# Zero-padded query tiles for the 64-wide heads of a two-layer hybrid trunk

## Chip, cores and metric

The kernel runs on one core of one Trainium2 chip. The metric is the device time of one execution in microseconds; before the change it is 2455.56 us, the median of 3 runs (2454.08 to 2456.77).

## The reference, cut to what matters

Two layers of an encoder trunk work on 512 prompt frames and 32 sample frames with a model width of 1024. A layer is a SwiGLU block, a mixer with three groups of attention heads side by side, a second SwiGLU block and a gated embedding. The mixer projects its normed input once and splits it:

```python
qa, ka, va, cq, ckv, kr, qc, kc, vc, fl = jnp.split(xn @ w_in, SPLITS, axis=-1)
qa, ka, va = (a.reshape(bsz, t, H_A, HEAD_DIM) for a in (qa, ka, va))     # 4 heads x 64
qc, kc, vc = (a.reshape(bsz, t, H_C, HEAD_DIM) for a in (qc, kc, vc))     # 4 heads x 64
...
z = jnp.einsum('bqhd,bkhd->bhqk', q, k).astype(jnp.float32) * SB_SCALE    # group A
z = jnp.einsum('bqhd,bkhd->bhqk', q, k).astype(jnp.float32) * MLA_SCALE   # group B, 96 wide, 8 heads
z = jnp.einsum('bqhd,bkhd->bhqk', q, k).astype(jnp.float32) * FOX_SCALE   # group C, plus a bias of forget gates
```

Group A is stick-breaking attention, B latent attention, C attention with forget gates. The scores of a head of A or C are sums over 64 products. Prompt frames see only earlier frames (or chunks), so a block of 128 queries needs 128, 256, 384 or 512 keys.

## The kernel before, in words

Activations lie transposed, features on partitions and the 544 frames along the row; the frames are worked on in two halves of 256 and 288 (HALVES). A projection (gemm, L238 to L240) is done as three passes over high and low parts of inputs and weights: each of 8 chunks takes three matmuls, so 24 for a half.

In the mixer, class QK projects 128 columns of W_in at a time, which are two heads of Q or of K, one head on partitions 0 to 63, the other on 64 to 127. VectorE evicts the result from PSUM with the norm's factor into one "m" buffer of 128x544 (L531 for K, L533 for Q, which also scales), ScalarE copies the sample frames to a small tile (L109, h<-m), and K is written out by a DMA that GpSimd issues (L537). Pool "m" has 14 buffers in this phase; besides Q and K of A and C it holds the latents of B (four tiles of cq, two of ckv), B's queries and parts of the normed output. A buffer is given to the next tile when all readers of its last one are done.

attend_qk takes the rows of each head out of the pair's tiles and calls attend_pair, which works on blocks of 128 queries. For each of the two heads it issues the score product (L395), for C a bias product (L401), the mask as a bf16 product with an identity (L402), the softmax or stick-breaking weights (soft, on ScalarE and VectorE), transposes (L135) and the product with V (L414). In A and C the score product of the second head is held in program order (hold); B's is not. B's heads have 128-row tiles of their own: 64 rows of content, 32 rotary rows and their 32 swapped ones. So L395 stands for 64-row products in A and C and 128-row products in B, all in float32. A float32 product shows up as two MATMUL records.

The program is written in dataflow form; a planner with modelled durations chooses the order on each engine and places the waits. Program order around the change: Q and K of A's first pair, its attention, Q and K of A's second pair, small projections, Q and K of C's first pair, A's second attention, C's first attention, Q and K of C's second pair, C's second attention, then B. The planner mixes projections, as far as they are ready, between the attention's products.

Of the kernel before, what the change touches and what calls it, by code (L numbers as in the profile page):

```python
# [12 lines left out]
ALU = mybir.AluOpType  # L13
# [5 lines left out]
SEQ = 512  # L19
DEC = 32  # L20
T = SEQ + DEC
# [14 lines left out]
def trunk(ctx: ExitStack, tc, a, outs, depth=2):  # L36
    nc = tc.nc
# [19 lines left out]
    def tl(tag, shape, dt=F32):  # L57
        count[0] += 1
        tag = alias.get(tag, tag)
        p, n = where[tag]  # L60
        return p.tile(shape, dt, tag=tag, name=f"{tag}_{count[0]}", bufs=n)
# [29 lines left out]
    unit = lambda tag, dt=F32: tl(tag, [128, T], dt)  # L91
# [5 lines left out]
    hold = tc.keep_in_program_order  # L97
# [4 lines left out]
    tt = nc.vector.tensor_tensor  # L102
    stt = nc.vector.scalar_tensor_tensor
    ts = nc.vector.tensor_scalar
    mm = nc.tensor.matmul
    f = lambda ap: ap.bitcast(F32)

    def copy(out, in_):
        act(out, in_, AF.Copy)  # L109
# [23 lines left out]
    def transpose(out, in_):  # L133
        n = in_.shape[0]
        nc.tensor.transpose(out, in_, ident[0:n, 0:n])  # L135
# [89 lines left out]
    def split_w(raw, k, n, parts=1):  # L225
        th, tlo = ring[wn[0] % len(ring)]
        wn[0] += 1
        hi, lo = tl(th, [128, k, n], F32R), tl(tlo, [128, k, n], F32R)
        for b in (slice(k * i // parts, k * (i + 1) // parts) for i in range(parts)):
            split(hi[:, b, :], lo[:, b, :], raw[:, b, :])  # L230
        return hi, lo

    def gemm(p, w, xh, xl, cols, order=None):
        wh, wl = w
        ks = order or list(range(len(xh)))
        c0, c1 = cols
        for i, k in enumerate(ks):
            mm(p, wh[k], xh[k][:, c0:c1], start=i == 0, stop=False)  # L238
            mm(p, wh[k], xl[k][:, c0:c1], start=False, stop=False)  # L239
            mm(p, wl[k], xh[k][:, c0:c1], start=False, stop=i == len(ks) - 1)  # L240

    def wk(w, n=128):
        return tuple([x[:, i, 0:n] for i in range(x.shape[1])] for x in w)
# [136 lines left out]
    def attend_pair(cb, kind, heads, o, chunk, vget, extra=None):  # L380
        identb = cb[:, 0:128]
        mask = cb[:, 128 * ("ABC".index(kind) + 1):128 * ("ABC".index(kind) + 2)]
        if chunk not in o:
            o[chunk] = unit("y")
        for b in range(2):
            cols = slice(b * 256, b * 256 + 256)
            O = tl("pv", [128, 256])
            pts = [tl("pb" if b else "pa", [128, 2 + 2 * b, 256]) for _ in heads]
            lqs = [extra(hd, cols) for hd, _ in heads] if extra else None
            for i in (2 * b, 2 * b + 1):  # L390
                nk, q0 = (i + 1) * 128, i * 128
                w = max(nk, 256) if extra else nk
                ss = [bank("acc") for _ in heads]
                for e, (_, (q, k)) in enumerate(heads):
                    one = mm(ss[e][:, 0:w], q[:, q0:q0 + 128], k[:, 0:w], start=True, stop=False)  # L395
                    if e and kind != "B":
                        hold(one)
                for e, s in enumerate(ss):
                    if extra:
                        lq, rk = lqs[e]  # L400
                        mm(s[:, 0:w], lq[0:100, q0 - b * 256:q0 - b * 256 + 128], rk[0:100, 0:w], start=False, stop=False)  # L401
                    mm(s[:, q0:nk], identb, mask, start=False, stop=True)  # L402
                    P = soft(kind, s[:, 0:nk], nk)
                    t = bank("tr")
                    for j in range(i + 1):
                        transpose(t[:, j * 128:j * 128 + 128], P[:, j * 128:j * 128 + 128])
                    qq = slice((i % 2) * 128, (i % 2) * 128 + 128)
                    (copy if e else nc.vector.tensor_copy)(pts[e][:, 0:i + 1, qq],
                                                           t[:, 0:nk].rearrange("p (j s) -> p j s", s=128))
            end = 2 * b + 1  # L410
            for j in range(end + 1):
                qs = slice(128 if j == end else 0, 256)
                for e, (hd, _) in enumerate(heads):
                    one = mm(O[64 * e:64 * e + 64, qs], vget(hd, j), pts[e][:, j, qs], start=j == 0, stop=j == end,  # L414
                             skip_group_check=True)
                    if j or e:
                        hold(one)
            (copy if b else nc.vector.tensor_copy)(o[chunk][:, cols], O)

    def soft(kind, S, nk):  # L420
        P = tl("t", [128, nk])
        if kind == "A":
            act(P, S, AF.Abs)
            act(P, P, AF.Exp, scale=-1.0)
            act(P, P, AF.Ln, bias=1.0)
            stt(P, S, 0.0, P, op0=ALU.max, op1=ALU.add)
            nc.vector.tensor_tensor_scan(P[:, ::-1], ones_row(0, 128, nk), P[:, ::-1], 0.0, op0=ALU.mult, op1=ALU.add)
            tt(P, S, P, op=ALU.subtract)
            act(P, P, AF.Exp)
        else:  # L430
            mx, sm = col(), col()
            nc.vector.reduce_max(mx, S, axis=AX.X, negate=True)
            act(P, S, AF.Exp, bias=mx, accum_out=sm)
            nc.vector.reciprocal(sm, sm)
            act(P, P, AF.Copy, scale=sm)
        return P
# [42 lines left out]
    def mix(l, h, x, g_next):  # L479
# [27 lines left out]
        sn = tl("h", [128, 8, DEC])  # L507
# [4 lines left out]
        def proj(col0):  # L512
            return wk(load_w(a["w_in"][l, UNITS.index(col0)], KD, 128))
# [3 lines left out]
        class QK:  # L517
            def __init__(s, col0, scale, slot, dst=None):
                s.col0, s.scale, s.slot, s.dst, s.w = col0, scale, slot, dst, None

            def half(s, i, pbank=prj):
                c0, c1 = HALVES[i]
                if s.w is None:
                    s.w = proj(s.col0)
                    s.kf = unit("m")
                n = c1 - c0
                p = pbank()[:, 0:n]
                gemm(p, s.w, x.xh, x.xl, (c0, c1))
                t = s.kf[:, c0:c1]
                if s.scale == 1.0:  # L530
                    tt(t, p, x.r(c0, c1), op=ALU.mult)  # L531
                else:
                    stt(t, p, s.scale, x.r(c0, c1), op0=ALU.mult, op1=ALU.mult)  # L533
                if c1 == T:
                    copy(sn[:, s.slot, :], s.kf[:, SEQ:T])
                    if s.dst is not None:
                        nc.gpsimd.dma_start(out=s.dst, in_=s.kf)  # L537

        def qk_jobs(qcol, kcol, scale, slot, dst):
            return [(QK(qcol + 128 * c, scale, slot + c),  # L540
# [30 lines left out]
        def attend_qk(kind, js, c, chunk, v, extra=None):  # L571
            q, k = js[c]
            heads = []
            for e in range(2):
                r = slice(e * 64, e * 64 + 64)
                heads.append((2 * c + e, tuple(z.kf[r, 0:SEQ] for z in (q, k))))
            attend_pair(cb, kind, heads, o, chunk, v.get, extra)

        def cache_kv(kname, vname):
# [71 lines left out]
        w = wk(split_w(raw, KD, 68), 68)  # L651
        for c0, c1 in HALVES:
            n = c1 - c0
            p = bank("prj")[0:68, 0:n]
            gemm(p, w, x.xh, x.xl, (c0, c1))
            t, u = tl("q", [128, n]), tl("q", [128, n])
# [4 lines left out]
            fx, e = t[64:68, :], u[64:68, :]  # L661
# [14 lines left out]
        w = proj(CKV)  # L676
        ckh, ckl, ckf = unit("m", F32R), unit("m", F32R), unit("kf")
        cks = unit("r")
        for c0, c1 in HALVES:
            p = bank("prj")[:, 0:c1 - c0]  # L680
# [7 lines left out]
        for c0, c1 in HALVES:  # L688
            R = tl("q", [128, c1 - c0])
# [5 lines left out]
        for c0, c1 in HALVES:  # L695
            R = tl("q", [128, c1 - c0])
# [147 lines left out]
        def attend_b(hp, q, k):  # L844
            heads = [(2 * hp + e, (q[e][:, 0:SEQ], k[e][:, 0:SEQ])) for e in range(2)]
            attend_pair(cb, "B", heads, o, 2 + hp, lambda hd, j: vb[j][:, hd * 64:hd * 64 + 64])
# [53 lines left out]
    def ple_inputs(l):  # L900
        ph, pl = ([unit("ph", F32R) for c in range(2)] for _ in range(2))
        for c in range(2):
            raw = unit("raw")
            nc.sync.dma_start(out=raw, in_=a["p"][l, c * 128:c * 128 + 128, :])
            split(ph[c], pl[c], raw)
        return ph, pl
# [87 lines left out]
    with phase(FFN, FFN_RING):  # L994
        h, x = start()
        x = ffn1(0, h, x)
    for l in range(depth):
        with phase(MIX, MIX_RING):
            h, x = mix(l, h, x, gains[l]["g_ff2_pre"])
        alias["h"], alias["y"] = alias.get("y", "y"), alias.get("h", "h")  # L1000
        with phase(FFN, FFN_RING):
            p = []
            x = ffn(h, x, a["w_ff2_gu"][l], a["w_ff2_down"][l], gains[l]["g_ff2_post"], gains[l]["g_ple_pre"], False,
                    lambda: p.extend(ple_inputs(l)))
            x = ple(l, h, x, gains[l + 1]["g_ff1_pre"] if l + 1 < depth else None, p)
            if l + 1 < depth:
                x = ffn1(l + 1, h, x)
# [99 lines left out]
```

## Time and profile before

| what | before |
|---|---|
| median of 3 runs | 2455.56 us |
| profiled execution | 2452.86 us, span 2451.1 us |
| granted TensorE clock, mean | 0.985 of full speed |
| PE (matmuls) | 2382.6 us, 97% of the span |
| PEld (weight loads, beside PE) | 2253.3 us, 92% |
| DVE (VectorE) | 1379.4 us, 56% |
| ACT (ScalarE) | 1025.6 us, 42% |
| POOL (GpSimd) | 48.8 us, 2% |

The span is the time from the first to the last instruction in the profiled execution; what lies outside it is 1.8 us. Matmuls overlap, and the profile models their ends, so the time that a matmul takes is better read from one start to the next than from its duration. The mixer of the first layer lies at 430 to 690 us and that of the second at about 1650 to 1910 us, in the same order of work.

### The profile page before, as it was taken

Reading aid. Unit: us, or ns where it says so; the run is one execution under the profiler, and the core shown is the slowest. Engines: PE = TensorE matmul, PEld = TensorE weight load, DVE = VectorE, ACT = ScalarE, POOL = GpSimd, SP = SyncE. Lnnn points to the kernel's source line nnn. Section 1 sums busy time; section 2 is a strip of 40 time slices with the busy share of each in tenths; the row PEclk is TensorE's granted clock in tenths of the full one; section 3 lists DMA queues with packets and bytes.
Section 4 is the critical chain, followed back from the end, with each engine's and each line's share of the span. In section 5 each row is a group of like instructions: output and inputs, shape, how many; then the busy total and the mean of one; then the engine's idle time right before and its main releaser. Section 6 shows DMA issues by size and latency. Waiting matters only on the chain.

```text
span 2451.1 us, 43918 instructions
## 1 busy us (share of the span) xinstructions
PE 2382.6 (97%) x18022; PEld 2253.3 (92%) x18022; DVE 1379.4 (56%) x3052; ACT 1025.6 (42%) x2163; POOL 48.8 (2%) x116
## 2 busy tenths in 40 slices
PE   8999999999998999999999999999999989999997
PEld 8999999886688999999999999998865989999997
DVE  6344446765757344446863444476667663444466
ACT  5322224566754322224533222245677543222243
POOL 0000000110000000000000000001100000000000
PEclk9999999999998999999999999999999999999998
DMA  5322322222023322322213223122211233323221
GB/s 160 111 81 86 105 70 72 93 88 59 23 80 107 104 88 83 101 85 87 84 47 96 95 80 102 54 94 86 89 51 44 81 94 105 95 75 104 81 70 37
DMA packets 72376, 204.99 MB, mean 84 GB/s; under 512 B 9248, under 2 KB 18088, under 8 KB 72176
## 3 DMA queue, kind: packets, MB, share of 16 engines
q1 hardware_dynamic: 69072, 193.57, 25.4%
q0 software_dynamic: 3104, 8.62, 1.1%
q8 instruction: 141, 2.31, 0.4%
q14 instruction: 59, 0.48, 0.1%
HBM read 188.21 MB, written 11.85 MB: 82 GB/s over the span
## 4 chain that ended last, share of the span: by engine, by line
PE 92%; DVE 4%; DMA 2%; ACT 1%; issue 0%; SPq 0%; DVEq 0%; ACTq 0%
PE acc L238 12%; PE acc L239 12%; PE acc L240 12%; PE prj L238 10%; PE prj L239 10%; PE prj L240 10%; PE pv L238 4%; PE pv L239 4%; PE pv L240 4%; PE acc L395 3%; PE pv L414 2%; PE tr L135 2%; DMA raw<-in_w_ff_gu_dram 1%; DVE z L303 1%; PE prj L556 1%; PE prj L557 1%
## 5 line engine op out<-in xcount | busy, mean ns | idle before, releaser
L109 ACT ACTIVATE wh<-raw 128x1024 fp32r<-128x1024 f32 (+3 forms) x157 | 151.1, 965 | 247.5 <-PE acc L239 108.1
L109 ACT ACTIVATE wx<-raw 128x1024 fp32r<-128x1024 f32 (+3 forms) x149 | 139.5, 936 | 266.4 <-PE acc L239 100.2
L113 DVE TENSOR_TENSOR wl<-raw,wh 128x1024 fp32r<-128x1024 f32 (+3 forms) x157 | 173.6, 1107 | 80.0 <-ACT wh L109 79.3
L113 DVE TENSOR_TENSOR wx<-raw,wx 128x1024 fp32r<-128x1024 f32 (+3 forms) x149 | 159.4, 1070 | 75.1 <-ACT wx L109 74.9
L238 PE MATMUL prj<-xa,wh 128*128 128x256 f32 (+3 forms) x632 | 187.8, 297 | 4.6 <-DVE q L346 2.7
L239 PE MATMUL prj<-xb,wh 128*128 128x256 f32 (+3 forms) x632 | 187.1, 296 | 4.1 <-DVE xb L259 4.1
L109 ACT ACTIVATE m<-q 128x256 fp32r<-128x256 f32 (+1 forms) x192 | 81.9, 431 | 255.0 <-DVE q L349 252.7
L240 PE MATMUL prj<-xa,wl 128*128 128x256 f32 (+3 forms) x632 | 184.3, 292 | 0.0
L238 PE MATMUL acc<-xa,wx 128*128 128x256 f32 (+1 forms) x600 | 174.4, 291 | 5.7 <-ACT wx L109 5.7
L239 PE MATMUL acc<-xb,wx 128*128 128x256 f32 (+1 forms) x600 | 173.8, 290 | 0.0
L240 PE MATMUL acc<-xa,wx 128*128 128x256 f32 (+1 forms) x600 | 173.4, 289 | 0.0
L239 PE MATMUL acc<-xb,wh 128*128 128x288 f32 (+1 forms) x576 | 167.4, 291 | 0.0
L240 PE MATMUL acc<-xa,wl 128*128 128x288 f32 (+1 forms) x576 | 166.8, 290 | 0.0
L238 PE MATMUL acc<-xa,wh 128*128 128x288 f32 (+1 forms) x576 | 166.6, 292 | 0.0
L240 PE MATMUL prj<-xa,wx 128*128 128x288 f32 (+1 forms) x480 | 139.5, 291 | 1.3 <-DVE wx L113 1.3
L238 PE MATMUL prj<-xa,wx 128*128 128x288 f32 (+1 forms) x480 | 140.6, 293 | 0.0
L239 PE MATMUL prj<-xb,wx 128*128 128x288 f32 (+1 forms) x480 | 140.3, 292 | 0.0
L347 ACT ACTIVATE q<-q 128x256 f32<-128x256 f32 (+1 forms) x176 | 74.1, 425 | 143.3 <-DVE q L346 140.8
L239 PEld LDWEIGHTS prj<-xb,wh 128*128 128x128 f32 (+1 forms) x632 | 120.1, 190 | 7.7 <-DVE xb L259 5.9
L238 PEld LDWEIGHTS prj<-xa,wh 128*128 128x128 f32 (+1 forms) x632 | 120.1, 190 | 7.7 <-DVE q L346 3.2
L240 PE MATMUL acc<-xa,wy 128*128 128x288 f32 (+1 forms) x424 | 122.7, 289 | 0.7 <-DVE wy L113 0.7
L238 PE MATMUL acc<-xa,wy 128*128 128x288 f32 (+1 forms) x424 | 123.3, 291 | 0.0
(500 smaller groups left out, 7802.5 us busy)
## 6 DMA issues: line engine op xcount, KB each, us to landing
raw<-in_w_ff_gu_dram SPq DMA_DIRECT2D x174, 512.0 KB, 3.5
raw<-in_w_ff_down_dram SPq DMA_DIRECT2D x64, 384.0 KB, 3.1
raw<-in_w_ff_down_dram SPq DMA_DIRECT2D x64, 320.0 KB, 2.9
raw<-in_w_in_dram SPq DMA_DIRECT2D x22, 512.0 KB, 3.5
raw<-in_w_out_dram SPq DMA_DIRECT2D x16, 512.0 KB, 3.4
raw<-in_w_ple_gate_dram SPq DMA_DIRECT2D x16, 512.0 KB, 3.4
raw<-in_w_v_dram SPq DMA_DIRECT2D x8, 512.0 KB, 3.4
t<-dh SPq DMA_DIRECT2D x16, 144.0 KB, 3.0
```

What stands on the lines that cost most here:

```text
L109: act(out, in_, AF.Copy)
L113: tt(lo, src, f(hi), op=ALU.subtract)
L135: nc.tensor.transpose(out, in_, ident[0:n, 0:n])
L238: mm(p, wh[k], xh[k][:, c0:c1], start=i == 0, stop=False)
L239: mm(p, wh[k], xl[k][:, c0:c1], start=False, stop=False)
L240: mm(p, wl[k], xh[k][:, c0:c1], start=False, stop=i == len(ks) - 1)
L303: stt(t, s.y[c][:, c0:c1], s.g[c], s.R[c0], op0=ALU.mult, op1=ALU.mult)
L347: act(g, g, AF.Silu)
L395: one = mm(ss[e][:, 0:w], q[:, q0:q0 + 128], k[:, 0:w], start=True, stop=False)
L414: one = mm(O[64 * e:64 * e + 64, qs], vget(hd, j), pts[e][:, j, qs], start=j == 0, stop=j == end, skip_group_check=True)
L556: mm(p, x.xh[k][:, c0:c0 + n], s.wh[k], start=k == 0, stop=False)
L557: mm(p, x.xl[k][:, c0:c0 + n], s.wh[k], start=False, stop=False)
```

## The change

Q of A and C gets a tile for each head instead of one for the pair. The head's 64 rows are written by the eviction, the other head's 64 rows are set to zero by a GpSimd memset. K keeps one tile for the pair. The score product of a head is then the product of its padded Q with the whole K tile, over 128 rows. The eviction of Q becomes two instructions of 64 partitions, the copy of the sample frames too. The hold on the second head's score product goes.

```diff
@@ attend_pair
                 for e, (_, (q, k)) in enumerate(heads):
-                    one = mm(ss[e][:, 0:w], q[:, q0:q0 + 128], k[:, 0:w], start=True, stop=False)
-                    if e and kind != "B":
-                        hold(one)
+                    mm(ss[e][:, 0:w], q[:, q0:q0 + 128], k[:, 0:w], start=True, stop=False)
@@ class QK
             def __init__(s, col0, scale, slot, dst=None):
                 s.col0, s.scale, s.slot, s.dst, s.w = col0, scale, slot, dst, None
+                s.rows = [slice(0, 64), slice(64, 128)] if dst is None else [slice(0, 128)]
 
             def half(s, i, pbank=prj):
                 c0, c1 = HALVES[i]
                 if s.w is None:
                     s.w = proj(s.col0)
-                    s.kf = unit("m")
+                    s.kf = [unit("m") for _ in s.rows]
+                    if len(s.rows) == 2:
+                        for e in range(2):
+                            nc.gpsimd.memset(s.kf[e][s.rows[1 - e], 0:SEQ], 0.0)
                 n = c1 - c0
                 p = pbank()[:, 0:n]
                 gemm(p, s.w, x.xh, x.xl, (c0, c1))
-                t = s.kf[:, c0:c1]
-                if s.scale == 1.0:
-                    tt(t, p, x.r(c0, c1), op=ALU.mult)
-                else:
-                    stt(t, p, s.scale, x.r(c0, c1), op0=ALU.mult, op1=ALU.mult)
-                if c1 == T:
-                    copy(sn[:, s.slot, :], s.kf[:, SEQ:T])
-                    if s.dst is not None:
-                        nc.gpsimd.dma_start(out=s.dst, in_=s.kf)
+                R = x.r(c0, c1)
+                for t, r in zip(s.kf, s.rows):
+                    if s.scale == 1.0:
+                        tt(t[r, c0:c1], p[r, :], R[r, :], op=ALU.mult)
+                    else:
+                        stt(t[r, c0:c1], p[r, :], s.scale, R[r, :], op0=ALU.mult, op1=ALU.mult)
+                    if c1 == T:
+                        copy(sn[r, s.slot, :], t[r, SEQ:T])
+                if c1 == T and s.dst is not None:
+                    nc.gpsimd.dma_start(out=s.dst, in_=s.kf[0])
@@ attend_qk
             for e in range(2):
-                r = slice(e * 64, e * 64 + 64)
-                heads.append((2 * c + e, tuple(z.kf[r, 0:SEQ] for z in (q, k))))
+                heads.append((2 * c + e, (q.kf[e][:, 0:SEQ], k.kf[0][:, 0:SEQ])))
```

## Rows read from the trace of the kernel before

**Rows 1.** The page: busy time, share and instructions of each engine.
```profile
PE 2382.6 (97%) x18022; PEld 2253.3 (92%) x18022; DVE 1379.4 (56%) x3052; ACT 1025.6 (42%) x2163; POOL 48.8 (2%) x116
```

**Rows 2.** Busy time by stretch: length, engines, granted clock, DMA share, GB/s.
```profile
480.00:515.00 35.00, 35.00 (x270) 32.94 (x268) 27.26 (x54) 18.61 (x36) 6.77 (x23) 1.00 0.26 80
...
537.00:567.00 30.00, 30.00 (x186) 21.31 (x185) 15.67 (x36) 18.16 (x45) 1.27 (x3) 1.00 0.24 70
...
640.00:690.00 50.00, 44.44 (x260) 30.62 (x260) 41.01 (x119) 38.95 (x110) 0.00 (x0) 0.97 0.14 46
```

**Rows 3.** Waits of weight loads, 440 to 600 us: total us, times, longest.
```profile
PEld tr L135 <- ACT t L424: 1.1, 2, 0.5
...
PEld acc L395 <- DVE m L531: 0.2, 1, 0.2
```

**Rows 4.** The score line's records: min/median/max ns, starts, shapes.
```profile
L395 PE MATMUL acc<-m,m x128: 272/481/694, 456.4 to 1805.2; 64*128 64x256 f32 x48, 64*128 64x384 f32 x32, 64*128 64x512 f32 x32, 64*128 64x128 f32 x16
...
L395 PE MATMUL acc<-xb,m x128: 271/484/648, 593.3 to 1878.3; 128*128 128x128 f32 x32, 128*128 128x256 f32 x32, 128*128 128x384 f32 x32, 128*128 128x512 f32 x32
```

**Rows 5.** Timeline of PE, a 64-row product: start us, us, instruction.
```profile
459.63 0.28 PE L238 MATMUL prj<-xa,wh 128*128 128x256 f32 x1
459.83 0.70 PE L395 MATMUL acc<-m,m 64*128 64x256 f32 x2
460.46 0.23 PE L402 MATMUL acc<-cb 128*128 128x128 bf16 x1
...
460.70 0.28 PE L240 MATMUL prj<-xa,wl 128*128 128x256 f32 x1
```

**Rows 6.** Timeline of PE, a 128-row product of group B.
```profile
614.66 0.29 PE L240 MATMUL prj<-m,wl 128*128 128x288 f32 x1
614.80 0.59 PE L395 MATMUL acc<-xb,m 128*128 128x256 f32 x2
615.23 0.22 PE L402 MATMUL acc<-cb 128*128 128x128 bf16 x1
...
615.46 0.28 PE L768 MATMUL prj<-m,wh 128*128 128x256 f32 x1
```

**Rows 7.** Timeline of PE, group C: through score and bias to the mask.
```profile
548.17 0.28 PE L240 MATMUL prj<-xa,wl 128*128 128x256 f32 x1
...
549.23 0.23 PE L402 MATMUL acc<-cb 128*128 128x128 bf16 x1
...
570.62 0.28 PE L401 MATMUL acc<-rk,lq 100*128 100x256 f32 x1
570.75 0.23 PE L402 MATMUL acc<-cb 128*128 128x128 bf16 x1
```

**Rows 8.** Timeline of PE, two heads' products that start together.
```profile
569.19 0.70 PE L395 MATMUL acc<-m,m 64*128 64x256 f32 x4
569.83 0.50 PE L767 MATMUL prj<-wh,m 128*128 128x512 f32 x1
```

**Rows 9.** Timeline of PE, group B, from mask to mask over 384 columns.
```profile
605.39 0.22 PE L402 MATMUL acc<-cb 128*128 128x128 bf16 x1
...
606.15 0.22 PE L402 MATMUL acc<-cb 128*128 128x128 bf16 x1
```

**Rows 10.** Single instructions on VectorE, ScalarE and GpSimd, by line and shape.
```profile
L533 DVE SCALAR_TENSOR_TENSOR m<-prj,r x14: 418/450/459, 452.8 to 1766.7; 128x288 f32<-128x288 f32 x8, 128x256 f32<-128x256 f32 x6
...
L801 DVE COPY xb<-prj x16: 425/425/427, 579.6 to 1838.3; 64x256 f32<-64x256 f32 x16
...
L109 ACT ACTIVATE h<-m x8: 212/212/225, 453.7 to 566.3; 128x32 f32<-128x32 f32 x8
...
L645 POOL MEMSET bq<- 128x512 f32 x2 | 1.1, 548 | 0.0
```

**Rows 11.** Timelines of PE and VectorE: A's last score, C's next Q.
```profile
534.55 1.12 PE L395 MATMUL acc<-m,m 64*128 64x512 f32 x2
...
542.37 0.42 DVE L533 SCALAR_TENSOR_TENSOR m<-prj,r 128x256 f32<-128x256 f32 x1 [1.00 <-PE prj L240]
```

## The prediction

> **What bounds the kernel now.** I read the page's busy times first, then busy time by stretch, then the waits of TensorE's weight loads, then the score line and the timeline around single products. The page shows TensorE's matmuls (PE) busy for 2382.6 of 2451.1 us, VectorE for 1379.4 and GpSimd for 48.8 [rows 1]. Busy time alone doesn't prove a bound, so look where the change lies: the scores of groups A and C, at 456 to 587 us in the first layer and 1675 to 1805 us in the second. There PE is busy 35.00 of 35.00 and 30.00 of 30.00 us, while VectorE has 27.26 and 15.67 and ScalarE 18.61 and 18.16 [rows 2]. Only after 640 us does PE have holes: 44.44 of 50. The weight loads' waits between 440 and 600 us agree: the largest that another engine ends is 1.1 us in two pieces, and the evictions of Q and K make a score wait once, for 0.2 us [rows 3]. So in the stretch of the change the end of the layer is set by how fast PE gets through its own list, and what a score product takes there goes to the end of the span.
>
> **The scores, 64 rows against 128.** The score line has 128 MATMUL records on 64 rows (64 products of two records, 32 in a layer) and as many on 128 rows, those of group B, which multiply the same float32 shapes over all rows [rows 4]. So the trace of before holds the price of both forms.
>
> Take 256 columns. On 64 rows, from the start of the projection matmul ahead to the start of the second projection matmul behind: 459.63 to 460.70, 1.07 us [rows 5]. The same chain on 128 rows: 614.66 to 615.46, 0.80 us, and the matmul ahead has 288 columns there, not 256, which is 0.01 us more [rows 6]. So 64 rows cost 0.28 us more for the same product. Where it lies can be seen in the steps: the product starts 0.20 us after the matmul ahead instead of 0.13 to 0.14, and takes 0.63 us to the mask's product instead of 0.43. I read it as a fixed charge for going into 64-row form, between its two passes and out again, where a weight load finds no matmul to hide behind, and so take it for all widths.
>
> Where forget-gate scores go straight into the bias product (10 of 16 products of C in a layer), the charge runs on: 548.17 to 549.23 is 1.06 us up to the mask's product; in 128-row form it would be 0.12 for the matmul ahead, 0.43 for the product [rows 6] and 0.13 from bias to mask, 0.68 in all. That is 0.38, so 0.10 more than above [rows 7].
>
> I went through the timeline product by product. Of the 32 of a layer 4 stand in two pairs, where the heads' four records start together: the pair of 256 columns takes 0.64 us from its start to the next matmul [rows 8], with about 0.11 us of going in. Two 128-row products take 2 x 0.43 = 0.86: a loss of 0.11. The pair of 128 columns gains some 0.06. Together -0.05 in a layer. The other 28 products run alone.
>
> Eight of these 28 follow the short bf16 mask product. There 128 rows have a charge too: 605.39 to 606.15 is 0.76 us, less 0.055 for the mask and 3 x 0.215 for 384 columns leaves 0.06 [rows 9]. I take 0.05 off for each.
>
> Sum for a layer: 28 x 0.28 = 7.84; + 10 x 0.10 = 1.0; - 8 x 0.05 = 0.4; - 0.05: 8.4 us. Two layers: 16.8 us. The ends: 0.19 us for each of 28 (the steps inside the product alone) is 10.6; 0.38 for every one of them is 21.3.
>
> **What is added elsewhere.** Each of the four Q tiles of a layer is now evicted by two VectorE instructions on 64 partitions in place of one on 128, in both halves: 16 more in both layers. An instruction on 64 partitions is no shorter (0.425 us for 64x256, against 0.418 to 0.459 for Q's own), so 16 x 0.44 = 7.0 us, and ScalarE gets 8 more copies of 0.21 us, 1.7 us [rows 10]. VectorE's idle share in these stretches hides them; if the projections' PSUM banks came free later and PE ran out of others, they would cost up to 7.0. The nearest row says almost nothing: the existing evictions hold up a score for 0.2 us [rows 3]. I take 0.5 us, ends 0 and 7.0. If the softmax chains behind them became the bound, the price is the same 7.0.
>
> The zeros are 16 GpSimd memsets of 64x512; the nearest is 128x512 in 0.548 us, so 8.8 us on GpSimd [rows 10]. What is queued behind them there is output and cache DMA issue. GpSimd idles nearly all the time [rows 1], and the first zeros are wanted at 456.4 us [rows 4], some 25 us after the mixer has begun. Cost 0, upper end 8.8 if every one stood ahead of a score; below nothing it can't be.
>
> The dropped program-order hold on the second head's score only gives the planner more freedom. The trace can't price a new order; nearest are group B's scores, which have no hold and start the same way, in 0.13 us behind a projection [rows 6]. I take 0, and plus or minus 3 us.
>
> Sum against the profiled execution's own 2452.86 us: 2452.9 - 16.8 + 0.5 = 2436.6. The runs' median is 2.7 above that execution (2455.56), so 2439.3 us is the forecast, 16.3 us less.
>
> A rule speaks against it. The Trainium skill, TensorEngine Tiling (Key Properties and When to Use Tiling), says that a product over at most 64 rows should use half the array's rows, since two such tiles can run in parallel, up to twice as fast. The trace agrees for the 4 pairs that start together [rows 8], but the other 56 products have nothing in the other half, and there half the rows is the dearer form.
>
> **Rivals.**
> 1. Half of it doesn't arrive. In C's stretch PE's work is more entangled with the softmax: 30.00 busy, but VectorE has just been given more. If C's gain (14 x 0.28 + 1.0 = 4.9 us a layer) becomes waiting, 2439.3 + 9.8 = 2449. Against it: both other engines are idle over a third of that stretch [rows 2].
> 2. No change: evictions uncovered (7.0), and a rewritten order that leaves the remaining 9 us in the holes after 640 us, where PE waits already [rows 2]. About 2455. For it: the order of everything is planned anew; against it: nothing of the change lies in that stretch.
> 3. Slower: the buffers. Fourteen buffers hold Q, K and the latents ("m"). A Q now takes two. When C's second pair is projected, there would be 4 + 2 latents, 3 of C's first pair, 3 of A's second and 3 new ones: 15. If A's second pair isn't done by then, the projection of C's second pair must wait and can't fill PE beside C's first attention. That projection is 2 x 2 x 24 matmuls of 0.12 to 0.13 us, 12.1 us a layer; uncovered in both layers, 24.2 - 16.3: 2463. It decides from the moment at which the first of these Q's evictions comes before A's last scores. In the trace A's last score product starts at 534.55 and that eviction at 542.37 [rows 11], so there are 8 us in hand.
> 4. Slower by the pairs: were all 32 pairs run in parallel, a pair would cost about what one product costs now, and two 128-row products would add 0.11, 0.36 and 0.58 us at 256, 384 and 512 columns (two products of 0.43, 0.645 and 0.86, less one of 0.75, 0.93 and 1.14) and save 0.06 at 128. That is 1.0 us for each of A's four pairs of heads and 1.2 for each of C's, 8.6 us slower, 2464. Against it: the trace has 4 pairs in parallel of 32. It is the rule of the Trainium skill's TensorEngine Tiling taken at its word.
>
> **How the numbers follow.** Forecast 0.65, its own range 2433 to 2446 (the ends of the score price and the planner's 3 us). Rival 1: 0.14. Rival 2: 0.11. Rival 3: 0.07. Rival 4: 0.03. This kernel's measurements can tell 0.2%, 4.9 us, from no change: faster means below 2450.6, slower above 2460.5. The forecast and rival 1 are faster, 0.79; rival 2 is no change, 0.11; rivals 3 and 4 are slower, 0.10. The range that leaves about 2 in 10 out reaches from 2431 over the forecast and rival 1 to 2453.
>
> **What would show it.** All 256 score MATMULs have 128 rows; the product starts 0.11 to 0.14 us after the matmul ahead and a 256-column one takes 0.43 us. PE's stretch from the first score to the layer's group norms is 8 to 9 us shorter in each layer, and the rest of the trace keeps its length. GpSimd has 16 more memsets and VectorE 16 more evictions; no score waits for either by more than some tenths. It is wrong if scores wait for GpSimd or for a buffer, if the projections of C's second pair move behind C's first attention, or if PE gets new holes that VectorE or ScalarE end.

## The result, and the profile after

The changed kernel takes 2439.47 us (median of 4 runs, 2437.84 to 2440.52), against 2454.82 us (2452.18 to 2456.77) for the kernel before beside it: a ratio of 0.9939, 95% interval 0.9927 to 0.9952, or 15.3 us less. The forecast was 2439.3 us. The profiled span went from 2451.1 to 2435.6 us.

The page of the changed kernel, busy time by engine, against [rows 1]:

```profile
span 2435.6 us, 43986 instructions
...
PE 2367.7 (97%) x18022; PEld 2258.5 (93%) x18022; DVE 1386.3 (57%) x3068; ACT 1028.2 (42%) x2171; POOL 58.5 (2%) x132
```

TensorE has as many instructions as before and 14.9 us less busy time. VectorE and GpSimd have the 16 more that were counted, 6.9 and 9.7 us; ScalarE has 8 more, 2.6 us.

The score line of the changed kernel, by shape, against [rows 4]:

```profile
L395 PE MATMUL acc<-m,m x128: 270/484/648, 455.2 to 1791.2; 128*128 128x256 f32 x48, 128*128 128x384 f32 x32, 128*128 128x512 f32 x32, 128*128 128x128 f32 x16
```

All 128 records that were on 64 rows are on 128, and the longest is 648 ns, as in group B, where it was 694. The last of them starts 14.0 us earlier than before. Now one product between its neighbours, in the timelines of PE and then of the weight loads, and under them the weight loads around the product of [rows 5] in the kernel before:

```profile
457.97 0.28 PE L238 MATMUL prj<-xa,wh 128*128 128x256 f32 x1
458.09 0.59 PE L395 MATMUL acc<-m,m 128*128 128x256 f32 x2
458.52 0.22 PE L400 MATMUL acc<-cb 128*128 128x128 bf16 x1
458.55 0.36 PE L239 MATMUL prj<-xb,wh 128*128 128x256 f32 x1
458.75 0.28 PE L240 MATMUL prj<-xa,wl 128*128 128x256 f32 x1
```

```profile
457.86 0.19 PEld L238 LDWEIGHTS prj<-xa,wh 128*128 128x128 f32 x1
457.98 0.30 PEld L395 LDWEIGHTS acc<-m,m 128*128 128x128 f32 x2
458.31 0.10 PEld L400 LDWEIGHTS <-cb 128*128 128x128 bf16 x1
```

```profile
459.51 0.19 PEld L238 LDWEIGHTS prj<-xa,wh 128*128 128x128 f32 x1
459.83 0.29 PEld L395 LDWEIGHTS acc<-m,m 64*128 64x128 f32 x2
460.46 0.10 PEld L402 LDWEIGHTS <-cb 128*128 128x128 bf16 x1 [0.33 <-issue]
```

Read them as steps, from one start to another. The second projection behind starts 0.78 us after the one ahead (457.97 to 458.75), against 1.07: 0.29 less, and 0.28 was forecast. The product starts 0.12 us after the projection ahead and takes 0.43 us to the mask, both as forecast. The lower fences show where the difference sits. On 128 rows the score's load begins 0.11 us before its product and the mask's load 0.21 us before the mask, both while the matmul ahead still runs. On 64 rows the score's load begins with its own product (459.83), and the mask's waits 0.33 us for nothing that the profile shows and begins with the mask (460.46).

In group C the charge ran on into the bias. The same chain of the changed kernel, projection to mask, against [rows 7]:

```profile
536.54 0.28 PE L239 MATMUL prj<-xb,wh 128*128 128x256 f32 x1
536.66 0.59 PE L395 MATMUL acc<-m,m 128*128 128x256 f32 x2
536.90 0.47 PE L399 MATMUL acc<-rk,lq 100*128 100x256 f32 x1
537.21 0.23 PE L400 MATMUL acc<-cb 128*128 128x128 bf16 x1
```

0.67 us, against 1.06; 0.68 was forecast. Whether another engine became the bound is seen in the stretches (columns as in [rows 2]) and in the added instructions by line:

```profile
480.00:515.00 35.00, 35.00 (x270) 33.23 (x269) 27.89 (x58) 21.07 (x47) 8.42 (x25) 1.00 0.24 73
537.00:567.00 30.00, 30.00 (x198) 22.51 (x196) 14.27 (x34) 17.27 (x42) 2.38 (x4) 1.00 0.35 104
640.00:690.00 50.00, 45.24 (x298) 35.18 (x297) 38.51 (x103) 35.39 (x92) 0.00 (x0) 0.97 0.20 63
```

```profile
L527 POOL MEMSET m<- x16: 517/522/528, 412.7 to 1732.1; 64x512 f32 x16
...
L536 DVE SCALAR_TENSOR_TENSOR m<-prj,r x28: 409/446/461, 452.0 to 1766.1; 64x288 f32<-64x288 f32 x16, 64x256 f32<-64x256 f32 x12
```

PE still has no hole in either stretch of the scores. The additions take about what was counted for them (0.45 us an eviction, against 0.44; 0.52 us a memset, against 0.55), and no score's wait ends at one of them.

### The profile page after: what moved, and what is told of

Read it like the earlier page. It is cut to its first block, busy times and chain, and to the rows that moved or that the text cites. A ratio compares the mean times of both kernels' runs of the same rounds, so it can differ in the third digit from the quotient of the medians.

```text
span 2435.6 us, 43986 instructions
## 1 busy us (share of the span) xinstructions
PE 2367.7 (97%) x18022; PEld 2258.5 (93%) x18022; DVE 1386.3 (57%) x3068; ACT 1028.2 (42%) x2171; POOL 58.5 (2%) x132
## 4 chain that ended last, share of the span: by engine, by line
PE 91%; DVE 4%; DMA 2%; ACT 1%; issue 1%; SPq 0%; DVEq 0%; ACTq 0%
PE acc L238 12%; PE acc L239 12%; PE acc L240 12%; PE prj L238 10%; PE prj L239 10%; PE prj L240 10%; PE pv L238 4%; PE pv L239 4%; PE pv L240 4%; PE acc L395 3%; PE pv L412 2%; PE tr L135 2%; DMA raw<-in_w_ff_gu_dram 1%; DVE z L303 1%; PE prj L559 1%
## 5 line engine op out<-in xcount | busy, mean ns | idle before, releaser
L240 PE MATMUL acc<-xa,wy 128*128 128x288 f32 (+1 forms) x424 | 123.1, 290 | 0.7 <-DVE wy L113 0.7
L239 PE MATMUL acc<-xb,wy 128*128 128x288 f32 (+1 forms) x424 | 123.7, 292 | 0.0
```

## Experiments

The theory: a score product on 64 rows that stands alone among 128-row matmuls costs a fixed charge of about 0.28 us whatever its width, and that charge alone is the gain. The rivals: the gain comes from the new order of the work (the dropped hold among it); it would be larger but for the additions; or pairs that run side by side are the cheaper form after all. Ratios are to the kernel before, run beside each; the brackets behind a ratio are its 95% interval, and 0.0010 of a ratio is 2.5 us.

**The order: hold dropped alone, and hold kept.** The first is the kernel before with this edit, the second the changed kernel with it undone:

```diff
-                    one = mm(ss[e][:, 0:w], q[:, q0:q0 + 128], k[:, 0:w], start=True, stop=False)
-                    if e and kind != "B":
-                        hold(one)
+                    mm(ss[e][:, 0:w], q[:, q0:q0 + 128], k[:, 0:w], start=True, stop=False)
```

> The kernel before with one edit: the second head's score product is no longer held in program order; all products of groups A and C stay on 64 rows. Theory (a lone 64-row product carries a fixed charge of about 0.28 us): nothing is removed, 2455 us, within 3 us. Rival (the gain comes from the freedom in order that the dropped hold gives): 2440 to 2447 us.

> The changed kernel with the hold put back. Theory (64-row charge): all score products are on 128 rows, so 2439.5 us, within 3 us. Rival (dropped hold): most of the gain is gone, 2448 to 2455 us.

Measured: 0.9998 (0.9989 to 1.0007) and 0.9934 (0.9921 to 0.9947). The hold is worth nothing that can be measured, with the tiles or without. The traces say why: the first kernel's instructions stand in the order of the kernel before on all five engines, and the second's in that of the changed kernel. The hold changed no order here, so these two runs are repetitions of the kernels before and after, and the new order is tested by the next run.

**The additions without the form.** The changed kernel, tiles, zeros, evictions, copies and all, but each product reads only its head's 64 rows:

```diff
             for e in range(2):
-                heads.append((2 * c + e, (q.kf[e][:, 0:SEQ], k.kf[0][:, 0:SEQ])))
+                r = slice(e * 64, e * 64 + 64)
+                heads.append((2 * c + e, (q.kf[e][r, 0:SEQ], k.kf[0][r, 0:SEQ])))
```

> The changed kernel with its two tiles for each Q, its split evictions and its zeros, but the score products taken over the head's 64 rows alone. Theory: the charge is back and the additions cost 0 to 7 us, taken as 0.5: 2455.5 us, range 2453 to 2462; VectorE has 16 more evictions and GpSimd 16 more memsets. Rival (separate tiles or the new order bring the gain): 2440 to 2448 us.

Measured: 1.0003 (0.9995 to 1.0012). This run tells most. Its instructions stand in the same order as the changed kernel's on all five engines, so the two differ in the form of 64 products and in nothing else. Against 0.9939 (0.9927 in the repetition below) that form is worth 0.0064 or 0.0076 of 2453 us, 15.7 or 18.6 us and 0.25 or 0.29 a product; the intervals leave some 4 us either way. Additions and new order together cost between -1.2 and +2.9 us. PE in this kernel, at the product shown above:

```profile
459.19 0.28 PE L238 MATMUL prj<-xa,wh 128*128 128x256 f32 x1
459.40 0.70 PE L395 MATMUL acc<-m,m 64*128 64x256 f32 x2
460.03 0.23 PE L400 MATMUL acc<-cb 128*128 128x128 bf16 x1
460.07 0.36 PE L239 MATMUL prj<-xb,wh 128*128 128x256 f32 x1
460.27 0.28 PE L240 MATMUL prj<-xa,wl 128*128 128x256 f32 x1
```

Line by line the same chain: 1.08 us, against 0.78. It is the same at 512 columns, in the changed kernel and then in this one:

```profile
467.77 0.29 PE L238 MATMUL prj<-xa,wh 128*128 128x288 f32 x1
467.90 1.02 PE L395 MATMUL acc<-m,m 128*128 128x512 f32 x2
...
469.00 0.30 PE L240 MATMUL prj<-xa,wl 128*128 128x288 f32 x1
```

```profile
470.24 0.29 PE L238 MATMUL prj<-xa,wh 128*128 128x288 f32 x1
470.46 1.12 PE L395 MATMUL acc<-m,m 64*128 64x512 f32 x2
...
471.77 0.29 PE L240 MATMUL prj<-xa,wl 128*128 128x288 f32 x1
```

1.23 us against 1.53, 0.30 again. As the order is the same, all 64 products can be compared so, from the matmul ahead to the third start behind. In this order 54 stand alone. On 64 rows they cost 0.14 to 0.48 us more, 17.9 us together; the median is 0.30 us at 128 and at 256 columns, 0.34 at 384 and 0.33 at 512. The other 10 stand in five pairs, which are 0.8 us cheaper together on 64 rows. That leaves 17.1 us.

**The dose: A alone, C alone.** The tiles for one group, the other one left as before (the other group's hold and its choice of rows in attend_qk are left out here):

```diff
-                s.rows = [slice(0, 64), slice(64, 128)] if dst is None else [slice(0, 128)]
+                pad = dst is None and slot < 4          # C alone: slot >= 4
+                s.rows = [slice(0, 64), slice(64, 128)] if pad else [slice(0, 128)]
```

> The change for group A alone; C stays on 64 rows and keeps its hold. Theory (a charge for each lone 64-row product): 14 x 0.28 a layer less the small terms, 7.6 us less than before, 2446 us. Rival (the gain sits in the new order around C, or in some other part): 2453 or 2439 us.

> The change for group C alone; A stays on 64 rows and keeps its hold. Theory: 14 x 0.28 + 10 x 0.10 a layer less the small terms, 9.2 us less than before, 2444.5 us; the gains of A alone and C alone add up to that of both. Rival: the whole gain or none of it.

Measured: A alone 0.9969 (0.9959 to 0.9979), 7.6 us less; C alone 0.9962 (0.9950 to 0.9975), 9.3 us less. Together 16.9, so the two halves add up to the whole within the noise. Whether C's products, ten of which a layer go straight into a bias, are the dearer ones can't be told from these two runs: 1.7 us lie between them, and each interval spans 5 to 6.

**The charge by itself.** The changed kernel, with a product of two columns ahead of each of its 64 score products; the score product then overwrites what it wrote. It is on the head's 64 rows in one kernel, on all 128 in the other:

```diff
-                    mm(ss[e][:, 0:w], q[:, q0:q0 + 128], k[:, 0:w], start=True, stop=False)
+                    if kind != "B":
+                        r = slice(64 * e, 64 * e + 64)  # the other: slice(0, 128)
+                        mm(ss[e][:, 0:2], q[r, q0:q0 + 128], k[r, 0:2], start=True, stop=True)
+                    one = mm(ss[e][:, 0:w], q[:, q0:q0 + 128], k[:, 0:w], start=True, stop=False)
+                    if kind != "B":
+                        hold(one)
```

> The changed kernel with one extra product of two columns on the head's 64 rows ahead of each of the 64 score products of A and C (it writes what the score product then overwrites). With the next run, which has the same instructions in the same order, it measures the charge for 64-row form alone, with next to no columns. Theory (a fixed charge for going in, between the passes and out): 0.28 us each over the 128-row extra product, 18 us over the next run, 2471 us; 12 us over it if the part between the passes needs columns. Rival (64 rows are dearer in proportion to the columns): within 4 us of the next run.

> The changed kernel with one extra product of two columns on all 128 rows ahead of each score product of A and C. Theory: its two passes take as long as their weight loads, 2 x 0.11 us, 14 us in 64 of them: 2453 us. Rival for the pair of runs: as in the run before.

Measured: 2468.04 us with 64 rows (1.0062, 1.0047 to 1.0077) and 2450.88 with 128 (0.9995, 0.9986 to 1.0005), in the same order of instructions. The difference is 17.2 us over 64 products, 0.27 each. PE in the first, then in the second:

```profile
459.33 0.28 PE L240 MATMUL prj<-xa,wl 128*128 128x256 f32 x1
459.54 0.38 PE L397 MATMUL acc<-m,m 64*128 64x2 f32 x2
459.85 0.70 PE L398 MATMUL acc<-m,m 128*128 128x256 f32 x2
...
460.62 0.28 PE L239 MATMUL prj<-xb,wh 128*128 128x256 f32 x1
```

```profile
459.10 0.28 PE L240 MATMUL prj<-xa,wl 128*128 128x256 f32 x1
459.22 0.28 PE L397 MATMUL acc<-m,m 128*128 128x2 f32 x2
459.36 0.68 PE L398 MATMUL acc<-m,m 128*128 128x256 f32 x2
...
460.11 0.28 PE L239 MATMUL prj<-xb,wh 128*128 128x256 f32 x1
```

1.29 against 1.01 us: the 0.28 again, for two columns as for 256. The charge doesn't hang on the width. The 128-row extra product itself adds 0.23 us to this chain (1.01 against 0.78), near the 0.22 expected; by the times it is 0.27 (2450.88 less the 2433.43 below, over 64), and the intervals don't tell these apart.

**The pairs rule.** Three kernels put the heads' products side by side. In two of them both products of A and C are issued as one unit, before (64 rows) and after the change (128 rows):

```diff
-                for e, (_, (q, k)) in enumerate(heads):
-                    one = mm(ss[e][:, 0:w], q[:, q0:q0 + 128], k[:, 0:w], start=True, stop=False)
...
+                def scores():
+                    for e, (_, (q, k)) in enumerate(heads):
+                        mm(ss[e][:, 0:w], q[:, q0:q0 + 128], k[:, 0:w], start=True, stop=False)
+                if kind == "B":
+                    scores()
+                else:
+                    with tc.tile_critical():
+                        scores()
```

> The kernel before with the two heads' 64-row score products issued one right behind the other in groups A and C (32 pairs instead of 4). Theory, with the rule that two half-height products run side by side: every pair starts together and costs about what one product costs, 0.5 to 1.1 us less a pair by its width, 24 us less in all, 2430 us; if the pairs have to wait for a second free PSUM bank, 2430 to 2440. Rival (two half-height products don't overlap when each pass loads its own weights, or waits for banks eat it): 2445 us or more.

> The changed kernel with the two heads' score products issued one right behind the other, in the same way as in the run of pairs on 64 rows, which has holes of 0.6 to 1.9 us ahead of each pair. It tells what the pairing itself is worth from what that way of issuing costs. Theory (two 64-row products side by side take the time of one, two 128-row ones the sum): without the holes the 128-row pairs would cost 8.6 us more than the 64-row ones, so about 2492 us against 2483.6; the holes and the rest are the same in both. Rival (64 rows are dearer even in pairs): below 2483 us.

Measured: 1.0130 (1.0114 to 1.0146) and 1.0145 (1.0131 to 1.0159). Both are slower than either kernel. The first was to take 2430 us and takes 2483.63, so its theory failed and its rival came in. The second misses its expectation too: it is 0.0015 or 3.7 us above the first, not 8.6, and the intervals overlap. A pair of 512 columns in each, and the first kernel's waits of weight loads from 430 to 720 us (total, times, longest):

```profile
484.88 0.28 PE L240 MATMUL prj<-xa,wl 128*128 128x256 f32 x1
486.86 1.13 PE L396 MATMUL acc<-m,m 64*128 64x512 f32 x4 [1.70 <-DVE wl L113]
```

```profile
485.40 0.28 PE L240 MATMUL prj<-xa,wl 128*128 128x256 f32 x1
487.38 1.98 PE L396 MATMUL acc<-m,m 128*128 128x512 f32 x4 [1.70 <-DVE wl L113]
```

```profile
PEld acc L396 <- issue: 20.9, 17, 4.1
```

The pair itself is as the rule says, 1.13 us for two products that take 1.98 on 128 rows. But the unit is set off from the work around it, and PE stands idle ahead of it, 1.70 us here in both kernels. Of the 290 us from 430 to 720, PE is idle for 28.5 and 28.2 us in the two, against 8.7 in the kernel before. Why the second isn't 8.6 us above the first isn't shown: the two also differ in the order of their work and in the granted clock (0.977 to 0.979 in the first, 0.982 in the second). So this edit cannot price the pair against the wide form in a full PE.

So a third kernel, the changed one with pairs on 64 rows for 384 and 512 columns only, put side by side by a two-column product into the second head's bank and by program order:

```diff
+                side = kind != "B" and i >= 2
+                if side:
+                    mm(ss[1][:, 0:2], identb, mask[:, 0:2], start=True, stop=True)
                 for e, (_, (q, k)) in enumerate(heads):
+                    r = slice(64 * e, 64 * e + 64) if side else slice(0, 128)
...
+                    if side:
+                        hold(one)
```

> The changed kernel, but blocks with 384 and 512 keys take their two heads' products on 64 rows, side by side; a two-column product into the second head's bank goes ahead so that both banks are there, and 15 or 16 of the 16 pairs stand right behind each other. Theory: a pair of 384 columns saves 0.36 us and one of 512 0.58 us against two 128-row products, 7.5 us in 8 of each, less 16 x 0.1 to 0.15 us for the small product: 4 to 6 us less than the changed kernel, 2433 to 2435.5. Rival (waiting for a second bank, and going in and out of 64 rows, eat it): 2439 us or more.

Measured: 0.9935 (0.9921 to 0.9949), the same as the changed kernel; the expected 4 to 6 us don't show, though the interval of 3.4 us either way could hide a part of them. One pair of it:

```profile
464.97 0.28 PE L238 MATMUL prj<-xa,wh 128*128 128x256 f32 x1
465.18 0.92 PE L399 MATMUL acc<-m,m 64*128 64x384 f32 x4
466.02 0.44 PE L135 MATMUL tr<-cst,t 128*128 128x128 f32 x2
```

0.84 us to the next matmul, where two 128-row products of 384 columns take 2 x 0.645 = 1.29. All but one of the 16 pairs stand side by side. Yet from A's first score to B's last this profile is only 0.2 us shorter than the changed kernel's in the first layer and 2.5 in the second. Why the rest doesn't arrive is open: two banks must be free at once before a pair starts, and B's order moved too; no run tells these apart.

**The changed kernel again**, unedited, beside the two with extra products:

> The changed kernel itself beside the two runs with extra products, as their base on the same chip, and for the low-clock stretches of one more profile. Theory: 0.994 of the kernel before, 2439 us; if the stretches at the low clock differ by chance from one execution to the next, their sum is again somewhere between 58 and 68 us, and the span follows it by about half. Rival: the change itself lengthens them, and it is 68 us again, with a new stretch near 1140 us.

Measured: 2433.43 us (2433.21 to 2439.42), 0.9927 (0.9912 to 0.9942); its profiled span is 2432.2. It was run because the first profile of the change shows less at its end than in its scores. By the start times of the same instructions the changed kernel gains 10.1 us on the kernel before in the first mixer and 11.1 in the second: 21.2 us, of which the end has 15.5. The rest goes in the granted clock (the third column from the end). The kernel before at the same work, then the changed kernel 11 us earlier, then PE there:

```profile
1141.00:1151.00 10.00, 8.72 (x68) 8.43 (x67) 8.21 (x18) 5.29 (x11) 0.00 (x0) 1.00 0.54 191
1151.00:1158.00 7.00, 7.00 (x63) 7.00 (x62) 7.00 (x24) 4.73 (x13) 0.00 (x0) 1.00 0.27 95
```

```profile
1130.00:1140.00 10.00, 8.44 (x64) 8.15 (x64) 8.32 (x18) 4.99 (x9) 0.00 (x0) 0.98 0.54 196
1140.00:1147.00 7.00, 7.00 (x38) 7.00 (x38) 4.86 (x17) 3.65 (x11) 0.00 (x0) 0.53 0.22 78
```

```profile
1139.18 0.39 PE L238 MATMUL prj<-ph,wx 128*128 128x256 f32 x1 [1.39 <-ACT m L933]
...
1140.46 0.44 PE L239 MATMUL prj<-ph,wx 128*128 128x288 f32 x1
1140.70 0.44 PE L240 MATMUL prj<-ph,wx 128*128 128x288 f32 x1
```

After a wait of 1.39 us for ScalarE the clock fell to its lower level (1.2 GHz of 2.4) for 6.8 us, the matmuls stood 0.24 us apart instead of 0.13, and 38 were done in 7 us where the kernel before did 63. The lead of the same instructions over the kernel before fell from 11.4 to 8.1 us there, and to 5.3 after a longer such stretch at 1239 us. In the repetition the first one is missing: the lead stays at 10.3 us from one mixer to the other, and the span is 18.9 us shorter. The kernel with the hold dropped, which has the order of the kernel before, does have such a stretch at 1150.5 us, again behind a wait of 1.39 us; the run with A alone has a wait of 1.38 us at the same place and no fall. So whether this one stretch comes is chance of the execution.

The mean over many executions is another matter. The 14 of the changed kernel's order (4 beside the result, 5 with the hold kept, 5 here) have a mean granted clock of 0.9833, the 48 of the kernel before beside the experiments 0.9851. That is about 8 us more at the lower level; at the 3.3 us that the stretch of 6.8 us cost, an estimate of some 4 us that the change loses again on average. The kernel with tiles and 64-row products has 0.9835 (mean of 11), so it goes with the tiles or their order and not with the form. Why is open.

## Why the prediction was right

**The bound.** That PE sets the end of the scores' stretch held: it has 35.00 and 30.00 us busy before and after, and between A's first score and C's last no gap at all in either kernel, so what is taken off a product comes off the stretch. The two doses, 7.6 and 9.3 us, add up to 16.9.

**The size.** 16.8 us were forecast for the scores. The pair of kernels that differ in the form alone has 15.7 to 18.6 by their times and 17.1 product by product; the extra products cost 0.27 each, where 0.28 was taken from [rows 5] and [rows 6]. C's dearer price is borne out by its own chain (0.67 against a forecast 0.68). The reading behind it, a fixed charge and not one per column, is shown by the two-column products and by the like charges from 128 to 512 columns. It was sized a little low: the 28 lone products of a layer were given 0.30 us each on average, terms for the bias and the mask included, and the 54 compared above cost 0.33. That the charge lies in weight loads that find no cover agrees with both timelines of loads, but no run took the load apart from the product, and these rows can't tell it from a pause of TensorE itself at each change of form: that part is argued.

**The additions.** Taken as 0.5 of 0 to 7.0 us (zeros 0 of 0 to 8.8); measured, together with the new order, -1.2 to +2.9. No score waited for an eviction or a memset. A cost of the additions alone, apart from what the order gave and the clock took, was not measured.

**The order.** The dropped hold was taken as 0 within 3 us. That held (0.9998), because the hold changed no order. The tiles did: 12 matmuls a layer that stood behind C's last score now stand ahead of it (848 matmuls from A's first score to C's last became 860; 448 from there to B's last became 436). So the gain has to be read over both stretches together. From A's first score to B's last both layers went from 203.4 to 193.9 us, 9.5 less each, where the sum had 8.4; up to the layers' group norms it is 10.1 and 11.1, where 8 to 9 were forecast. The kernel with tiles and 64-row products, in the same new order, takes 203.6 and 200.3: the order alone gave nothing in the first layer and 3.1 us in the second, where four pairs stand side by side instead of two, and the form the rest.

**What was luck.** That the median lies 0.2 us from the forecast is luck. The same instructions in the same order took 2437.66 and 2433.43 us in the two repetitions. In the trace the two layers' stretches from A's first score to B's last gave 19.1 us, not 16.8, and "the rest of the trace keeps its length" was wrong: the changed kernel's lower mean clock, which no term of the sum held, took some of it back. The two misses, of some 2 and 4 us, worked against each other.

**The rivals.** No score waits for a buffer: A's last score starts at 527.77 us and C's second Q is evicted from 538.73, 11.0 us in hand (rival 3); C's half came in full (1); no new holes (2). The rule that spoke against the change is half right. The Trainium skill's TensorEngine Tiling (Key Properties) says that different tiles can execute in parallel, and the trace agrees where two products do start together: 0.84 us against 1.29 at 384 columns. But the kernel before had 4 such pairs of 32, and of the ways tried to have more one left PE idle for 20 us more in the first layer's mixer and was slower, and the other gained nothing that shows in the time. The rule speaks of a pair; this change was decided by products that were alone.

## What to carry to other kernels

A product that uses half the rows isn't half the work, nor free, when its neighbours use all: look at the starts of the matmuls around it, not at its own duration, and take the same shape on all rows elsewhere in the trace as the price of the other form. Zeros that make it full height are a cheap trade where PE is full and the engine that writes them idles. Before counting on two half-height products side by side, count in the trace how many start together, and what an order that forces them makes PE wait for. And compare stretches that hold the same instructions: a new order can move work from one stretch to the next and look like a gain in one of them.

## What the runs showed of the hardware

- A lone 64-row float32 product among 128-row matmuls cost about 0.3 us more than a 128-row one at every width that stands here: 0.27 with 2 columns, and medians of 0.30 to 0.34 from 128 to 512 columns.
- A product of two columns on 128 rows is not free either: it added 0.23 us to its chain, and 64 of them made the kernel 17.5 us slower.
- The time that a profile shows at the lower clock level, leaving out the stretch that ends the span, varied between executions: 58.0 us in the kernel before, 68.3 in the changed kernel, 61.4 in its repetition. A wait of 1.39 us ahead had a fall behind it in two executions and one of 1.38 us had none in a third, so a difference of 3 to 6 us between two single profiles of this kernel can come from this alone.
